# Attention and recurrent layer: output stores shared between two queues, weights split in halves, one gated output split later

## The chip, the cores and the metric

The kernel runs on one core of a Trainium2 chip. The metric is the device time of one launch in microseconds. A core has TensorE (PE, matmuls; its weight loads are listed as PEld), VectorE (DVE), ScalarE (ACT), GpSimd (POOL) and SyncE (SP, which here only issues DMAs). Each engine works through its own instructions in the order in which they stand in the program, and waits for the others by semaphores.

## What is computed

One step of a decoder trunk over a prompt of 1024 tokens and 8 sample tokens, model width 1024. The trunk has two layers: a recurrent block and its MLP, then a sliding-window attention and its MLP. Every sub-layer is normed first and added to the residual stream. The two mixers, cut to what matters:

```python
def recurrent_block(x, h0, conv_prev, w_in, ...):
    gate, xr = jnp.split(x @ w_in, 2, axis=-1)
    xc, conv_new = causal_conv(xr, conv_prev, conv_w, conv_b)
    y, h_new = rg_lru(xc, h0, w_a, b_a, w_x, b_x, lam)      # sigmoid gates, then a scan over time
    return (y * jax.nn.gelu(gate)) @ w_out, h_new, conv_new

def qkv_heads(x, w_qkv, q_g, k_g):
    q, k, v = jnp.split(x @ w_qkv, ...)                      # 16 query heads, 4 key/value heads of 64
    return rms_norm(q, q_g), rms_norm(k, k_g), v

def sink_attention(q, k, v, dist, mask, sinks):              # window of 128 positions
    s = jnp.einsum('...qkgd,...skd->...kgqs', q, k) * (HEAD_DIM ** -0.5)
    s = jnp.where(mask, s - slopes * dist, NEG_INF)
    m = jnp.maximum(jnp.max(s, axis=-1, keepdims=True), sink)
    e = jnp.exp(s - m)
    p = e / (jnp.sum(e, axis=-1, keepdims=True) + jnp.exp(sink - m))
    return jnp.einsum('...kgqs,...skd->...qkgd', p, v)
```

## The kernel before

All 1032 tokens stand in the columns of tiles, 128 rows of the model width to a tile, so that one activation is eight tiles of 128x1032. A matmul works on a third of the columns (344, chunks c = 0, 1, 2). To keep float32 accuracy each operand is held as a rounded part and a remainder (`hi`, `lo`; for weights `wh`, `wl`), and each product is three matmuls: hi by hi, lo by hi, hi by lo. So everything that PE reads is first split: ACT casts the rounded part (`act.copy`) and DVE subtracts it from the source to give the remainder.

**Weights.** They come in units of 128x1024. SP loads a unit into one of two raw buffers, ACT casts `wh` (L179), DVE makes `wl` (L180), which frees the raw buffer. `unit(n, j, ahead)` returns a unit and sees to it that the next `ahead` units are split as well. The first four units of the program are split in two halves of 512 columns, all others whole.

**Recurrent layer** (to about 335 us). `LRU` is a list written out by hand that sets the order of stages: x (projections of the recurrent branch), c (convolution), g (sigmoid gates of a block, L1309), r (Tanh, Exp, squares and scan), o (`gate_out`: projection of the gate branch, Gelu, product with the scanned y, and the split of the result into `goh` on ACT and `gol` on DVE, for the output projection). The stretch that matters reads `o0 o1 o3 g3 r3 o6 o2 o4 o7`. A scheduler orders instructions by their readiness and priority within each engine's queue, so code that is moved also moves neighbours. Sigmoid, Gelu, Sqrt and Exp make ACT load other tables (`ACT_TABLE_LOAD`).

**Attention** (about 985 to 1250 us). `proj_many` makes the first key and query tile, `v_proj` the values; the other seven query tiles and the second key tile are filler, put between the matmuls of attention. `q_evac` empties each chunk of a query tile (square on ACT, L839; `hi` L841, `lo` on DVE L842, then stored to four half tiles by SP). One step of attention: scores in a bank bS (L963), the biased minimum on DVE (L973), the exponential on ACT (`se`, L976), the reciprocal on DVE (L978), the scaling on GpSimd (L980), transposes on PE (L990) and their copy `pt` (L997), and the product with the values in bO (L1013). `stage_c` closes a group of four steps: for each of two head tiles, u = 0 and 1, ACT casts the output `o` (L1020), DVE makes its remainder (L1021), and for the first four head tiles (t < 4) both go to DRAM tensors `od` (od0h is the rounded part of head tile 0, od1l the remainder of head tile 1), to be loaded again for the output projection. There are eight such groups, with four stores each. `S` buffers (128x344) come from a ring of nine; a buffer is used again once everything that read it is done, a store included.

Of the kernel before, what the change touches and what calls it, by code (L numbers as in the profile page):

```python
# [65 lines left out]
def trunk(ctx: ExitStack, tc: tile.TileContext, I, O):  # L66
    nc = tc.nc
    pe, act, dve, pool, sp = nc.tensor, nc.scalar, nc.vector, nc.gpsimd, nc.sync
# [33 lines left out]
    def A2(s="a"):  # L102
        return ap.tile([P, TW], F32, tag="A", name=nm(s))

    def A(s="a"):
        return A2(s)[:, 0:T]
# [4 lines left out]
    def S(s="s"):  # L111
        return small["pool"].tile([P, CH], F32, tag="S", name=nm(s))
# [5 lines left out]
    def B(tag=None):  # L118
        if tag is None:
            tag = ring[turn[0] % len(ring)]  # L120
            turn[0] += 1
        return psum["pool"].tile([P, 512], F32, tag=tag, bufs=BANKS[tag], name=nm("b" + tag))
# [14 lines left out]
    def r_(x):  # L137
        return x.bitcast(F32R)

    def cs(c):  # L140
        return slice(c * CH, (c + 1) * CH)
# [11 lines left out]
    def V(n, m=0):  # L153
        o, _ = VEC[n]
        return vec[:, o + m:o + m + 1]
# [10 lines left out]
    def fetch(n):  # L166
        while len(raws) < min(n, len(units)):
            name, _, src, _ = units[len(raws)]
            if name[:2] == "dn":
                raws.append(small["pool"].tile([P, RQ[int(name[2])]], F32, tag="Q", name=nm("raw")))  # L170
            else:
                raws.append(R("raw"))
            sp.dma_start(raws[-1][:, 0:src.shape[1]], src)

    def split_unit(raw, alloc, eng, parts=1):
        hi, lo = alloc("wh"), alloc("wl")
        for q in range(parts):
            sl = slice(q * D // parts, (q + 1) * D // parts)
            act.copy(r_(hi[:, sl]), raw[:, sl])  # L179
            eng.tensor_tensor(r_(lo[:, sl]), raw[:, sl], hi[:, sl], ALU.subtract)  # L180
        return hi, lo
# [8 lines left out]
    for o in [("x", m) for m in range(4)] + LRU:  # L190
        if o[0] == "g":
            units.append(("gate", o[1], I["w_gate"][o[1]], W))
        elif o[0] in "xo":
            m = o[1] + (8 if o[0] == "x" else 0)
# [13 lines left out]
    nloaded = [0]  # L208

    def ensure(k):  # L210
        while nloaded[0] <= min(k, len(units) - 1):
            n, j, _, alloc = units[nloaded[0]]
            fetch(nloaded[0] + (NRAW[int(n[2])] if n[:2] == "dn" else 2))
            if alloc is None:
                loaded[(n, j)] = raws[nloaded[0]]
            else:
                loaded[(n, j)] = split_unit(raws[nloaded[0]], alloc, pool if nloaded[0] in (3, 13) else dve,
                                            2 if nloaded[0] < 4 else 1)
            nloaded[0] += 1

    def unit(n, j, ahead=2):
        k = index[(n, j)]
        for _ in range(ahead):
            if k + 1 < len(units) and units[k + 1][3] is not None:
                k += 1
        ensure(k)
        return loaded.pop((n, j))
# [26 lines left out]
    def proj(w, xs, **kw):  # L254
        ps = banks3()
        mm_group(ps, w, xs, range(NCH), **kw)
        return ps
# [8 lines left out]
    def split_act_dve(hi, lo, src, sl, eng=dve):  # L266
        act.copy(r_(hi[:, sl]), src)
        eng.tensor_tensor(r_(lo[:, sl]), src, hi[:, sl], ALU.subtract)
# [237 lines left out]
    class PairWeights:  # L506
# [13 lines left out]
        def source(self, key, name):  # L520
            kind, q = key
            if key not in self.src:
                n = f"{kind}{self.layer}"
                ensure(index[n, 2 * q + 1])
                xy = []
                for t in (loaded.pop((n, 2 * q)), loaded.pop((n, 2 * q + 1))):
                    w = P * (4 if kind == "up" else len(self.chunks[q // 4]))
                    xy += [t[0][:, 0:w], t[1][:, 0:w]] if isinstance(t, tuple) else [t[:, 0:w], t[:, w:2 * w]]
                self.src[key] = {"w": w, **dict(zip(("A21", "A11", "A12", "A22"), xy))}
            src = self.src[key]  # L530
            if name not in src:
                w = src["w"]
                x, y, op = SUMS[name]
                x, y = self.source(key, x), self.source(key, y)
                if name in ("S1", "S3"):
                    src[name, 1] = W("ws")
                src[name] = src[("S1" if name in ("S1", "S2") else "S3"), 1][:, slice(w, 2 * w) if name in ("S2", "S4") else slice(0, w)]
                dve.tensor_tensor(src[name], x, y, op)  # L538
            return src[name]
# [250 lines left out]
    def attention(hs):  # L790
# [114 lines left out]
        def vblk(b, p):  # L905
            h = b // 4
            o = (b % 4) * 256 + p * P
            return v_tiles[h][:, o:o + P]
# [91 lines left out]
        def stage_c(g):  # L1000
            t, b0 = STEPS[4 * g]
            p = t // 4
            op = B("O")
            for n in range(2):
                y = live.pop(("pt", 2 * g + n))
                b = b0 + n
                first = 1 if b == 0 else 0
                o = op[:, n * 256:n * 256 + 256]
                for h in range(first, 2):
                    x = vblk(b - 1 + h, p)  # L1010
                    for u in range(2):
                        r = slice(64 * u, 64 * u + 64)
                        pe.matmul(o[r, :], lhsT=x[:, r], rhs=y[:, (2 * h + u) * 256:(2 * h + u) * 256 + 256],  # L1013
                                  start=h == first, stop=h == 1, tile_position=(0, 64 * u))
            dst = slice(b0 * P, (b0 + 2) * P)
            for u in range(2):
                src = op.rearrange("p (b t q) -> p b t q", b=2, t=2)[:, :, u, :]
                x = [S("o")[:, 0:2 * P] for _ in range(2)] if t < 4 else [y[:, dst] for y in ohl[t + u]]
                hi, lo = [y.rearrange("p (b q) -> p b q", b=2) for y in x]
                last["o"] = act.copy(r_(hi), src).ins  # L1020
                dve.tensor_tensor(r_(lo), src, hi, ALU.subtract)  # L1021
                if t < 4:
                    for d, y in zip(od[t + u], x):
                        sp.dma_start(d[:, dst], y)

        kc, vc, zs = [], [], []

# [128 lines left out]
        for j in range(NJ):  # L1156
# [6 lines left out]
            n = max(0, int((j + 1 - j1) * r) - int((j - j1) * r)) if j < J0 or j >= J1 else 0  # L1163
            if j and j % 4 == 0:
                stage_c(j // 4 - 1)
# [9 lines left out]
            if J0 <= j < J0 + 4:  # L1175
                ensure(index["wo1", j - J0])
# [8 lines left out]
            if j == 52:  # L1185
                for t in range(4):
                    load_o(t, slice(2 * CH, SEQ))
        stage_c(NJ // 4 - 1)

        for _ in fill:  # L1190
# [107 lines left out]
    rr = {}  # L1298

    def gates(kb):  # L1300
        w = unit("gate", kb, 3)
        xk = [xcs[2 * kb], xcs[2 * kb + 1]]
        for mm in range(2):
            for g, b in ((0, "ba"), (1, "bx")):
                ps = proj(w, xk, col=lambda k: k * 512 + g * 256 + mm * P)
                o = A("ri")
                with tc.high_priority():
                    for c in range(NCH):
                        act.activation(o[:, cs(c)], ps[c], AF.Sigmoid, bias=V(b, 2 * kb + mm))  # L1309
                rr[2 * kb + mm, g] = o  # L1310
# [31 lines left out]
    def gate_out(m):  # L1342
        ps = proj(unit("in", m, 3 if ("o", m) != LRU[-1] else 0), hs)
        y = ys.pop(m)
        for c in range(NCH):
            g = S("g")
            dve.tensor_tensor(g, ps[c], rx[:, cs(c)], ALU.mult)
            act.activation(g, g, AF.Gelu_apprx_tanh)
            dve.tensor_tensor(y[:, cs(c)], y[:, cs(c)], g, ALU.mult)
        hi, lo = A("goh"), A("gol")  # L1350
        split_act_dve(hi, lo, y, slice(0, T))
        gos[m] = (hi, lo)

    stages = {"x": xr_stage, "c": conv, "g": gates, "r": recur, "o": gate_out}
    xr_first()
    for what, i in LRU:
        stages[what](i)
        if (what, i) == ("r", 3):
            sp.dma_start(O["states"], st)
    gl = [gos[m] for m in range(M8)]  # L1360
# [131 lines left out]
def _build(arrays):  # L1492
    import concourse.bacc as bacc

    nc = bacc.Bacc("TRN2", target_bir_lowering=False, num_devices=1)
    I = {n: nc.dram_tensor(n, a.shape, mybir.dt.from_np(a.dtype), kind="ExternalInput").ap() for n, a in arrays.items()}
    O = {n: nc.dram_tensor("o_" + n, s, F32, kind="ExternalOutput").ap() for n, s in _OUT_SHAPES.items()}
    with tile.TileContext(nc) as tc:
        trunk(tc, I, O)
    return nc  # L1500
# [23 lines left out]
```

## Time and profile before

| | us |
|---|---|
| median of 3 runs (1973.4 to 1975.09) | 1974.5 |
| the profiled execution | 1974.77 |
| its span, first to last instruction | 1973.0 |
| PE busy | 1959.7 |
| DVE busy | 1499.1 |
| ACT busy | 1007.2 |
| GpSimd busy | 357.4 |

A profile is one execution. A timeline row gives the start, the duration, the engine, the line, the operation and its tiles (out<-in), and in brackets how long the engine had stood idle before it and what ended that. `x4` folds four neighbours into one row. The mean granted clock of PE was 0.999.

### The profile page before, as it was taken

The page shows a single profiled execution, that of the slowest core. Times are in us where ns is not written, and L with a number is a line of the kernel's source. Part 1 is how long each engine was busy: PE and PEld are TensorE (multiplying, and loading weights), DVE is VectorE, ACT ScalarE, POOL GpSimd, SP SyncE. Part 2 cuts the span into 40 slices and gives each one's busy share as a digit, 9 for nine tenths or more (in the row PEclk, how much of TensorE's full clock was granted, in tenths as well). Part 3 has the DMA queues.
Part 4 walks back from the last instruction along what each step waited for, and adds up shares of the span by engine and source line. Part 5 has one row for each costly group of instructions (what it writes and reads, how often), then busy time and mean ns, then how long its engine had stood idle before and what let it go on. Part 6 is the DMA issues. An engine that isn't in the chain of part 4 may idle for free.

```text
span 1973.0 us, 34782 instructions
## 1 busy us (share of the span) xinstructions
PE 1959.7 (99%) x13004; PEld 1826.8 (93%) x13004; DVE 1499.1 (76%) x2996; ACT 1007.2 (51%) x1964; POOL 357.4 (18%) x614
## 2 busy tenths in 40 slices
PE   9999999999999999999999999999999999999999
PEld 8999999999999899999999897999999999999998
DVE  8996647987777888777846768579877779688784
ACT  6576535543434655544545657456443436455552
POOL 2220000000001233321005647100000003223321
PEclk9999999999999999999999999999999999999999
DMA  5111242244445798988344435612444447788877
GB/s 183 54 44 54 65 159 83 108 151 156 144 152 196 215 244 209 239 204 199 111 110 108 131 94 186 216 62 97 165 140 156 141 176 261 202 203 219 229 201 180
DMA packets 116441, 308.07 MB, mean 156 GB/s; under 512 B 17448, under 2 KB 47152, under 8 KB 116272
## 3 DMA queue, kind: packets, MB, share of 16 engines
q0 software_dynamic: 29472, 102.06, 21.6%
q1 hardware_dynamic: 58576, 133.44, 20.7%
q10 hardware_dynamic: 28224, 70.35, 10.0%
q8 instruction: 102, 1.67, 0.4%
q14 instruction: 67, 0.55, 0.1%
HBM read 177.95 MB, written 115.15 MB: 149 GB/s over the span
## 4 chain that ended last, share of the span: by engine, by line
PE 92%; DVE 3%; issue 2%; DMA 1%; ACT 1%; POOL 0%; SPq 0%; DVEq 0%; ACTq 0%; POOLq 0%
PE bD L570 35%; PE bZ L570 26%; PE bP L240 11%; PE bS L240 6%; PE bP L890 5%; PE bT L240 3%; PE bO L1013 2%; PE bS L963 1%; PE bS L920 1%; PE bT L990 1%; DVE xc L1281 1%; PE bP L990 1%; DMA x<-xT 0%; DVE wl L180 0%; PE bN L854 0%
## 5 line engine op out<-in xcount | busy, mean ns | idle before, releaser
L570 PEld LDWEIGHTS bD<-op,op 128*128 128x128 f32 x3072 | 380.5, 188 | 7.8
L570 PE MATMUL bD<-op,op 128*128 128x260 f32 x3072 | 383.0, 282 | 0.0
L570 PEld LDWEIGHTS bD<-tl,op 128*128 128x128 f32 x2880 | 362.3, 188 | 12.7 <-DVE ho L718 1.4
L570 PE MATMUL bD<-tl,op 128*128 128x260 f32 x2880 | 366.6, 282 | 0.8 <-DVE ho L718 0.7
L583 POOL DMA_DIRECT2D tl<-hsum x210 | 124.3, 670 | 892.8 <-PE bD L570 412.6
L417 ACT CAST op<-ws 128x512 fp32r<-128x512 f32 (+2 forms) x288 | 158.7, 560 | 248.8 <-DVE ws L538 123.2
L570 PE MATMUL bZ<-op,op 128*128 128x512 f32 x1152 | 282.2, 394 | 0.0
L570 PE MATMUL bZ<-tl,op 128*128 128x512 f32 x1080 | 272.0, 395 | 0.5 <-DVE tl L425 0.2
L570 PEld LDWEIGHTS bZ<-op,op 128*128 128x128 f32 x1152 | 210.5, 188 | 43.6 <-ACT he L704 0.4
L570 PEld LDWEIGHTS bZ<-tl,op 128*128 128x128 f32 x1080 | 194.3, 188 | 38.3 <-DVE tl L425 0.8
L425 DVE TENSOR_TENSOR tl<-tl 128x520 fp32r<-128x520 f32 (+1 forms) x210 | 136.5, 691 | 75.0 <-ACT tl L424 74.1
L417 ACT CAST op<-raw 128x512 fp32r<-128x512 f32 (+2 forms) x216 | 120.8, 561 | 135.0 <-PE bD L570 73.1
L418 DVE TENSOR_TENSOR op<-ws,op 128x512 fp32r<-128x512 f32 (+2 forms) x288 | 171.0, 609 | 9.7 <-ACT op L417 9.5
L418 DVE TENSOR_TENSOR op<-raw,op 128x512 fp32r<-128x512 f32 (+2 forms) x216 | 131.3, 609 | 9.7 <-ACT op L417 8.8
L718 DVE TENSOR_TENSOR ho<-bD,ho 128x520 f32<-128x520 f32 x140 | 97.3, 695 | 38.8 <-PE bD L570 37.2
L424 ACT CAST tl<-tl 128x520 fp32r<-128x520 f32 (+1 forms) x210 | 117.9, 626 | 3.8 <-DMA tl<-hsum 2.2
L708 DVE TENSOR_TENSOR ho<-bZ,ho 128x512 f32<-128x512 f32 x72 | 49.5, 687 | 44.6 <-PE bZ L570 44.3
L180 DVE TENSOR_TENSOR wl<-raw,wh 128x1024 fp32r<-128x1024 f32 (+1 forms) x53 | 61.4, 1166 | 27.2 <-ACT wh L179 17.6
L966 POOL TENSOR_SCALAR bias<-con,st 128x256 f32<-128x256 f32 (+1 forms) x128 | 64.3, 503 | 86.4 <-DVE den L973 46.9
L710 ACT COPY he<-bZ 128x512 f32<-128x512 f32 x68 | 39.9, 586 | 77.3 <-PE bZ L570 65.7
L692 ACT COPY he<-bZ 128x512 f32<-128x512 f32 x72 | 41.9, 582 | 71.4 <-PE bZ L570 65.0
L718 DVE TENSOR_TENSOR he<-bD,he 128x520 f32<-128x520 f32 x71 | 49.4, 695 | 38.1 <-PE bD L570 37.7
(347 smaller groups left out, 3941.6 us busy)
## 6 DMA issues: line engine op xcount, KB each, us to landing
raw<-w_up SPq DMA_DIRECT2D x64, 512.0 KB, 4.2
tl<-hsum POOLq DMA_DIRECT2D x120, 260.0 KB, 6.5
raw<-w_dn SPq DMA_DIRECT2D x64, 384.0 KB, 6.5
tl<-hsum POOLq DMA_DIRECT2D x90, 256.0 KB, 6.5
spill<-ho POOLq DMA_DIRECT2D x32, 516.0 KB, 6.7
spill<-he POOLq DMA_DIRECT2D x32, 516.0 KB, 6.4
hsum<-ts ACTq DMA_DIRECT2D x30, 520.0 KB, 3.7
hsum<-ho ACTq DMA_DIRECT2D x30, 516.0 KB, 3.5
```

What stands on the lines that cost most here:

```text
L180: eng.tensor_tensor(r_(lo[:, sl]), raw[:, sl], hi[:, sl], ALU.subtract)
L240: pe.matmul(o, lhsT=r_(wt[:, col(k):col(k) + P]), rhs=r_(xt[:, cs(c)]), start=(k == first and a == 0), stop=(k == final and a == 2))
L417: act.copy(r_(hi), x)
L418: dve.tensor_tensor(r_(lo), x, hi, ALU.subtract)
L424: act.copy(r_(hi), lo)
L425: eng.tensor_tensor(r_(lo), lo, hi, ALU.subtract)
L570: pe.matmul(d[:, 512 * b:512 * b + c], lhsT=r_(wt[:, j * P:j * P + P]), rhs=r_(xt[:, c * b:c * b + c]), start=first and j == 0 and a == 0, ...
L583: pool.dma_start(t[:, n:2 * n], src)
L708: dve.tensor_tensor(o0, d, o[:, HP], ALU.add)
L718: last["sum"] = dve.tensor_tensor(t, inner(d), t, ALU.add).ins
L890: pe.matmul(o, lhsT=r_(wt[:, k * P:k * P + P]), rhs=r_(xt[:, cs(c)]), start=(k == 0 and a == 0), stop=(k == M8 - 1 and a == 2))
L966: pool.tensor_scalar(bias2[:, o - n:o], distM[:, 256 - n:256], fac[:, t % 4, 1, b, u:u + 1], SLOPES[hd[u]], ALU.mult, ALU.mult)
```

## The change

1. In `stage_c` the two stores of the second head tile (u = 1: od1h, od1l, od3h, od3l) are issued by ACT, not SP. Those of u = 0 stay on SP.
2. The units of q, k, v and the output weights of the attention layer (`wo1`), 20 in all, are split in two halves of 512 columns.
3. The second gate block (kb = 1) asks for one unit ahead, not three.
4. For gate output 3 the split into `goh` and `gol` is put off until the next stage that isn't a gate output has been written, which is g3.

```diff
-                                            2 if nloaded[0] < 4 else 1)
+                                            2 if nloaded[0] < 4 or n in ("q", "k", "v", "wo1") else 1)
...
                     for d, y in zip(od[t + u], x):
-                        sp.dma_start(d[:, dst], y)
+                        (act if u else sp).dma_start(d[:, dst], y)
...
     def gates(kb):
-        w = unit("gate", kb, 3)
+        w = unit("gate", kb, 1 if kb == 1 else 3)
...
             dve.tensor_tensor(y[:, cs(c)], y[:, cs(c)], g, ALU.mult)
+        if m in (3,):
+            owed.append((m, y))
+        else:
+            gate_split(m, y)
+
+    def gate_split(m, y):
         hi, lo = A("goh"), A("gol")
         split_act_dve(hi, lo, y, slice(0, T))
         gos[m] = (hi, lo)
+
+    owed = []
...
         stages[what](i)
+        if what != "o" and owed:
+            gate_split(*owed.pop())
```

**At g3, on ACT.** Before, behind o3's three Gelus (L1348); `goh` is the cast of o3's output, `ri` are the sigmoids of g3, which empty PE's banks bP, bS and bT:

```order
L1348 ACTIVATE g_1976<-g_1976 128x344
L267 CAST goh_1980<-t_1211 128x1032
L1309 ACT_TABLE_LOAD
L1309 ACTIVATE ri_2011<-bP_1990,vec 128x344
L1309 ACTIVATE ri_2036<-bS_2015,vec 128x344
L1309 ACTIVATE ri_2011<-bP_1991,vec 128x344
```

Now the table load follows the Gelus:

```order
L1348 ACTIVATE g_1976<-g_1976 128x344
L1309 ACT_TABLE_LOAD
L1309 ACTIVATE ri_2007<-bP_1986,vec 128x344
L1309 ACTIVATE ri_2007<-bP_1987,vec 128x344
L1309 ACTIVATE ri_2007<-bP_1988,vec 128x344
```

and the cast stands behind the last of the twelve sigmoids, ahead of r3's Tanh (L1321) and Exp (L1323):

```order
L1309 ACTIVATE ri_2082<-bT_2063,vec 128x344
L267 CAST goh_2086<-t_1205 128x1032
L179 CAST wh_2230<-raw_2131 128x1024
L1321 ACTIVATE t_2093<-ri_2057,sp_333 128x1032
L1323 ACT_TABLE_LOAD
L1323 ACTIVATE ri_2057<-ri_2057,vec 128x1032
```

The sigmoids also stand in another order, one product after the other.

**At the norm ahead of the first key and query products, on ACT.** L306 to L308 are the norm's factor, `hh` the rounded parts of the normed activation, L839 the square of a query chunk. Before:

```order
L306 ACTIVATE q_10419<-bN_10410,vec 128x344
L179 CAST wh_10771<-raw_10763 128x1024
L307 ACTIVATE r_10418<-q_10419 128x344
L308 ACTIVATE q_10419<-r_10418 128x344
L839 ACTIVATE sq_10579<-bT_10639 128x344
L267 CAST hh_9874<-t_10425 128x344
```

Now:

```order
L306 ACTIVATE q_10419<-bN_10410,vec 128x344
L179 CAST wh_10779<-raw_10769 128x512
L307 ACTIVATE r_10418<-q_10419 128x344
L179 CAST wh_10779<-raw_10769 128x512
L308 ACTIVATE q_10419<-r_10418 128x344
L267 CAST hh_9874<-t_10425 128x344
L839 ACTIVATE sq_10585<-bT_10645 128x344
```

The cast of the weight is in two pieces, and the first `hh` has changed places with the square.

**At the fourth group of stores.** On ACT the group reads now as follows (before, the two DMA rows weren't there); `hi` is a query chunk, `se` an exponential:

```order
L1020 CAST o_12095<-bO_12080 128x256
L1024 DMA od1h<-o_12095 128x256
L1024 DMA od1l<-o_12096 128x256
L841 CAST hi_12173<-bP_12075 128x344
L976 ACTIVATE se_10474,den_10467<-se_10474,den_10467 128x257 x2
```

On DVE, a little later in the same place, before:

```order
L1021 TENSOR_TENSOR o_12233<-bO_12225,o_12232 128x256
L1021 TENSOR_TENSOR o_12239<-bO_12225,o_12238 128x256
L842 TENSOR_TENSOR lo_12252<-bP_12161,hi_12251 128x344
L973 ISA se_10475,den_10469<-bS_12246,bias_10473,nsink,st 128x256
L973 ISA den_10469 128x1
```

and now:

```order
L1021 TENSOR_TENSOR o_12253<-bO_12245,o_12252 128x256
L1021 TENSOR_TENSOR o_12259<-bO_12245,o_12258 128x256
L973 ISA se_10475,den_10469<-bS_12266,bias_10473,nsink,st 128x256
L973 ISA den_10469 128x1
L973 ISA se_10475,den_10469<-bS_12266,bias_10473,nsink,st 128x256
L973 ISA den_10469 128x1
L842 TENSOR_TENSOR lo_12272<-bP_12181,hi_12271 128x344
```

The remainder of the query chunk (L842) has moved behind the two softmax steps (L973).

## The prediction

> **What bounds the kernel now.** I read the page first, then the stretches, then the timeline where TensorE stands still.
>
> ```profile
> span 1973.0 us, 34782 instructions
> PE 1959.7 (99%) x13004; PEld 1826.8 (93%) x13004; DVE 1499.1 (76%) x2996; ACT 1007.2 (51%) x1964; POOL 357.4 (18%) x614
> 140.00:190.00 50.00, 50.00 (x319) 50.00 (x318) 40.08 (x59) 30.53 (x41) 0.83 (x2) 1.00 0.19 64
> 985.00:1005.00 20.00, 19.03 (x117) 18.02 (x115) 14.89 (x28) 12.13 (x26) 0.00 (x0) 1.00 0.25 80
> 1120.00:1140.00 20.00, 18.86 (x141) 17.35 (x141) 13.51 (x52) 11.30 (x36) 10.00 (x21) 1.00 0.61 174
> 1180.00:1200.00 20.00, 19.01 (x140) 15.84 (x139) 15.49 (x63) 13.55 (x43) 11.47 (x25) 1.00 0.60 171
> 1200.00:1220.00 20.00, 20.00 (x143) 16.84 (x144) 18.73 (x79) 13.83 (x44) 17.34 (x33) 1.00 0.66 221
> ```
>
> TensorE (PE) is busy 1959.7 of 1973.0 us, and the change leaves every matmul in place. So only what PE stands idle for can be won: 13.3 us in all. The stretches (start and end, length, then the busy time of PE, weight loads, VectorE, ScalarE, GpSimd) put about 1 us of it at each of three places that the change touches: 0.97 at 985, 1.14 at 1120 and 0.99 at 1180. Between 1200 and 1220 PE has no gap, but VectorE (DVE) is busy 18.73 of 20 us there. The rest of the change is worth what it does to those waits, or what new waits it makes.
>
> The profiled execution took 1974.77 us (span 1973.0 and 1.8 around it), 0.27 above the median of 1974.5. I sum against 1974.77 and take off 0.27 at the end.
>
> **The gate output that is split later (g3).** The rows are from the timeline of ScalarE (ACT) and of PE.
>
> ```profile
> 185.96 1.34 ACT L1348 ACTIVATE g<-g 128x344 f32<-128x344 f32 x3 [0.23 <-DVE g L1347]
> 188.03 1.06 ACT L267 CAST goh<-t 128x1032 fp32r<-128x1032 f32 x1 [0.73 <-DVE t L1349]
> 189.10 1.28 ACT L1309 ACT_TABLE_LOAD   x1
> 190.40 0.55 ACT L1309 ACTIVATE ri<-bP,vec 128x344 f32<-128x344 f32 x1
> 190.01 0.32 PE L240 MATMUL bT<-xch,wl 128*128 128x344 f32 x1
> 191.00 0.43 PE L240 MATMUL bP<-xch,wh 128*128 128x344 f32 x1 [0.67 <-ACT ri L1309]
> 191.26 0.32 PE L240 MATMUL bP<-xcl,wh 128*128 128x344 f32 x1
> 191.42 0.32 PE L240 MATMUL bP<-xch,wl 128*128 128x344 f32 x1
> ```
>
> ACT ends its Gelus at 187.30, waits 0.73 for DVE, casts for 1.06, loads a table for 1.28, and only then empties the first bank with a sigmoid. PE stood for that bank: matmuls of 344 columns start 0.16 apart (191.26, 191.42), so the one at 191.00 was due at 190.17 and is 0.83 late. With the cast behind all twelve sigmoids, the table load can follow the Gelus: 187.30 + 1.28 = 188.58, and the first sigmoid ends near 189.1, a microsecond before PE wants the bank. Gain 0.8; bounds 0 (another wait behind it) and 0.83. The moved cast and its DVE half now lie ahead of Tanh and Exp of r3, but that chain starts up to 1.8 us earlier (0.73 + 1.06), which covers them; the split gate output itself is first read in the output projection, after the remaining gate outputs. Uncovered, the cast would cost 1.06.
>
> **Weights one unit later (second gate block).** The cast that leaves the second gate block turns up later, between Exp and the squares of r2, where DVE waits for ACT:
>
> ```profile
> 136.91 1.05 ACT L179 CAST wh<-raw 128x1024 fp32r<-128x1024 f32 x1 [3.34 <-DMA raw<-w_in]
> 138.45 0.86 PE L240 MATMUL bP<-hh,wh 128*128 128x344 f32 x2 [0.37 <-ACT ri L1309]
> 152.84 2.65 DVE L1329 SCALAR_TENSOR_TENSOR t<-a,t 128x344 f32<-128x344 f32 x6 [4.13 <-ACT a L1328]
> ```
>
> The units stay in their order, each split in the place of its successor, so the cast at 136.91 will handle the unit before and wait for a load freed by the same DVE step; PE's wait at 138.45 stays. The extra cast, 1.05 like the one at 136.91, pushes r2's DVE chain back by up to as much. PE has no gap from 140 to 190, so the trace shows no slack and no lack of it. I take 0, with bounds of +1.05 and, if the wait at 138.45 goes, -0.37.
>
> **Weights of the attention layer in halves.** 20 units become two casts and two subtractions each. The place that matters is the norm ahead of the first key and query products:
>
> ```profile
> 988.46 0.55 ACT L306 ACTIVATE q<-bN,vec 128x344 f32<-128x344 f32 x1 [1.88 <-PE bN L277]
> 988.91 1.04 ACT L179 CAST wh<-raw 128x1024 fp32r<-128x1024 f32 x1
> 992.80 0.46 ACT L839 ACTIVATE sq<-bT 128x344 f32<-128x344 f32 x1 [1.94 <-PE bT L240]
> 993.15 1.23 ACT L267 CAST hh<-t 128x344 fp32r<-128x344 f32 x3
> 989.98 1.23 DVE L180 TENSOR_TENSOR wl<-raw,wh 128x1024 fp32r<-128x1024 f32 x1 [2.10 <-ACT wh L179]
> 993.75 1.36 DVE L268 TENSOR_TENSOR hl<-t,hh 128x344 fp32r<-128x344 f32 x3
> 992.45 0.32 PE L240 MATMUL bT<-hh,wl 128*128 128x344 f32 x1
> 993.68 0.58 PE L240 MATMUL bP<-hh,wh 128*128 128x344 f32 x2 [0.91 <-ACT hh L267]
> L417 ACT CAST op<-raw 128x512 fp32r<-128x512 f32 (+2 forms) x216 | 120.8, 561 | 135.0 <-PE bD L570 73.1
> L418 DVE TENSOR_TENSOR op<-raw,op 128x512 fp32r<-128x512 f32 (+2 forms) x216 | 131.3, 609 | 9.7 <-ACT op L417 8.8
> ```
>
> PE was due at 992.45 + 0.16 = 992.61 and is 1.07 late. In the new order the first cast hh stands ahead of the square of L839, so it can start at 992.80 instead of 993.15: 0.35 earlier. DVE's 1.23 becomes two pieces that can start half a cast sooner. But hl at 993.75 is close behind and PE needs it next; DVE sets that. I take 0.4, bounds 0 and 1.07. Two halves cost ACT 2 x 0.561 - 1.04 = 0.08 more per unit and DVE 2 x 0.609 - 1.23, nothing. Over 20 units that is 1.6 us of ACT, spread over stretches in which ACT is busy 11.3 to 13.8 of 20 us: no cost, and 1.6 without that cover.
>
> **Half of the output stores on ACT.** Sixteen of 32 stores leave SP's queue for ACT's. Rows of the timeline: SP, ACT, DVE, PE.
>
> ```profile
> 1116.27 2.62 SPq L877 DMA_DIRECT2D kl<-x  x4
> 1120.09 0.40 SPq L1024 DMA_DIRECT2D od1h<-o  x1
> 1114.93 0.37 ACT L1020 CAST o<-bO 128x256 fp32r<-128x256 f32 x1 [0.90 <-DVE o L1021]
> 1115.20 0.45 ACT L841 CAST hi<-bP 128x344 fp32r<-128x344 f32 x1
> 1115.37 0.42 DVE L1021 TENSOR_TENSOR o<-bO,o 128x256 fp32r<-128x256 f32 x1
> 1123.85 0.52 DVE L842 TENSOR_TENSOR lo<-bP,hi 128x344 fp32r<-128x344 f32 x1 [2.40 <-DMA od1h<-o]
> 1125.35 0.39 PE L963 MATMUL bS<-kh,q 128*128 128x256 f32 x1 [0.33 <-DVE den L973]
> 1128.76 0.39 PE L963 MATMUL bS<-kh,q 128*128 128x256 f32 x1 [0.81 <-DVE den L973]
> ```
>
> The piece stored as od1h is ready at 1115.30, but SP has key stores to issue first (the last four alone take 2.62, to 1118.89) and reaches it at 1120.09. Its buffer is wanted again by DVE's L842, which stands 2.40 us until 1123.85; behind it on DVE wait the softmax steps L973, and PE twice stands for them, 0.33 and 0.81. The idle time falls 0.16 short of a delay (0.67 listed against 0.83 at 191.00, 0.91 against 1.07 at 993.68), so the two make 0.33 + 0.81 + 2 x 0.16 = 1.5. In the new order ACT issues od1h right behind its cast, nearly 5 us earlier, and L973 stands ahead of L842. Both waits go: gain 1.5, bounds 0 and 1.5.
>
> What ACT pays: behind its second cast it issues one store, waits for DVE's remainder (1115.37 + 0.42 = 1115.79), and issues the next. The nearest ACT issue is
>
> ```profile
> L380 ACTq DMA_DIRECT2D spill<-y x48: 326/326/1086, 249.8 to 1330.8; - x48
> 1066.81 0.46 ACT L839 ACTIVATE sq<-bP 128x344 f32<-128x344 f32 x1 [0.48 <-PE bP L890]
> ```
>
> 0.33 each, so ACT is free at 1115.79 + 0.33 = 1116.12 instead of 1115.20: 0.9 us per group, 7.4 over eight groups. Queued behind are the cast hi, the exps and the copies pt of the transposed softmax tiles; DVE, GpSimd and PE wait for those in turn. Behind the first group ACT is idle 0.48 anyway. ACT has 5 us or more spare in these 20 us stretches and PE mostly runs behind it, so I charge 0.2 in all; bounds 0 and 7.4.
>
> [...]
>
> **The stop at 1197.**
>
> ```profile
> 1191.15 1.23 DVE L180 TENSOR_TENSOR wl<-raw,wh 128x1024 fp32r<-128x1024 f32 x1 [0.77 <-ACT wh L179]
> 1197.20 0.93 PE L990 MATMUL bT<-con,se 128*128 128x128 f32 x4 [0.93 <-POOL se L980]
> ```
>
> PE waits 0.93 at the end of a softmax chain through DVE, ACT and GpSimd. A weight in halves lets DVE start the first at about half the 0.77 it waits now. I take 0.5, bounds 0 and 0.93 + 0.16 = 1.09.
>
> **Sum.** -0.8 + 0 - 0.4 - 1.5 + 0.2 - 0.5 = -3.0: 1971.77 for an execution like the profiled one, 1971.5 as median.
>
> **Rivals.**
> - *Every touched wait goes.* 0.83 + 1.07 + 1.5 + 1.09 = 4.5 less, 1970.0, and 1969.5 if the wait at 138.45 goes as well. For: each has a named cause that the new order takes away. Against: hl close behind hh at 993.75, and the chain at 1197 has other links.
> - *The transfer, not its issue, holds the buffer, or DVE takes the gain back.* The store lands behind the key stores whoever issues it; or what was won is lost again at 1200 to 1220, where DVE has only 1.27 us spare. Then the 1.5 is missing: 1973.0.
> - *Slower: ACT's stores hold up softmax.* ACT takes its instructions in order, so a store that waits for DVE stops the exps behind it. The price is 0.9 us per group; with all of it on PE's path, and the sum's other terms of 1.7 kept without the 1.5, 7.4 - 1.7 = 5.7 more, 1980.2. It turns the sum positive once more than 3.2 / 8 = 0.4 us per group is uncovered. For: GpSimd and PE's transposes follow the exps closely (the 0.93 at 1197 is such a chain). Against: idle ACT behind the group at 1066. [...]
>
> **How the numbers follow.** Forecast 0.42, every wait gone 0.30, transfer or DVE 0.13, slower 0.15. A measurement of this kernel can tell about 0.2%, 3.9 us, from no change. Faster than 1970.6 takes the first rival and 0.12 of the forecast's share: 0.42. Slower than 1978.4 is mostly the last rival's: I give 0.11 to it and leave its other 0.04, with 0.30 and 0.13, within 0.2%: 0.47. The range runs from 1968.7, every wait gone and a microsecond more behind it, to 1976.5, where the stores cost about 5 us (2/3 of the bound) beside the other gains; beyond are about 0.06 below and 0.13 above.
>
> **What would show it.** Right: ACT's table load at g3 directly behind the Gelus and no wait of PE on ri near 190; no wait of DVE L842 on a store; PE busy 20.0 in the stretch that was 18.86. The halves are right if PE's wait before the first key product falls below 0.8. Wrong: PE waits on L973 or L980 right behind the store groups, ACT exps that start 0.5 us or more later than DVE's L973 ends, a new PE wait between 150 and 180, or L842 still waiting for a store that ACT issued early.

## The result, and the profile after

| | before | after |
|---|---|---|
| median of 21 runs each, us | 1974.68 | 1971.7 |
| lowest and highest, us | 1973.03, 1975.57 | 1970.23, 1976.66 |
| ratio, 95% interval | | 0.9987, 0.9981 to 0.9993 |

The highest run of after is one whose mean granted clock was 0.997; the other twenty had 0.999 or 1.0. The changed kernel is 3.0 us faster (by the interval 1.4 to 3.8), less than the 3.9 us that the prediction named as the bound for telling it from no change. From the page of after, and its stretches with the columns of the prediction:

```profile
PE 1959.2 (99%) x13004; PEld 1826.8 (93%) x13004; DVE 1500.5 (76%) x3016; ACT 1008.8 (51%) x1984; POOL 358.3 (18%) x614
985.00:1005.00 20.00, 19.25 (x119) 18.11 (x118) 14.21 (x28) 11.99 (x28) 0.00 (x0) 1.00 0.27 86
1120.00:1140.00 20.00, 20.00 (x153) 18.95 (x152) 15.03 (x60) 12.76 (x40) 11.96 (x24) 1.00 0.52 148
1180.00:1200.00 20.00, 19.02 (x140) 15.13 (x138) 15.76 (x67) 13.07 (x41) 12.18 (x27) 1.00 0.65 188
```

Of the three gaps in these stretches one has closed (PE 18.86 before, 20.00 now), one has shrunk a little (19.03, now 19.25), one is as it was (19.01, now 19.02).

To see what each place gave, I set every PE instruction of one trace beside the same instruction of the other, wherever PE had done the same work up to it, and took the difference of their starts. How much that difference grows over a stretch is what the stretch gave. Where nothing was changed it moves too. Over the second feed-forward layer after gains 0.4 and the stores alone 1.3, of which 0.9 is one wait of PE at 1728 that some executions have and others don't. Over the first, after loses 0.6 in many small pieces; every kernel with all the parts loses 0.5 to 0.8 there and the stores alone lose nothing, so this belongs to the kernel, and its cause is open. Single places are good to a tenth or two, the sum of an execution is not. Gains against before, in us (stretches by the start in before):

| stretch | predicted | after | stores alone | halves alone | late split alone |
|---|---|---|---|---|---|
| 187 to 214, g3 | 0.8 | 0.94 | 0.03 | 0.03 | 1.04 |
| 975 to 995, norm ahead of keys and queries | 0.4 | 0.17 | 0 | 0.18 | 0 |
| 1104 to 1110 | not foreseen | -0.44 | -0.43 | -0.74 | 0 |
| 1124 to 1134, the store group | 1.5 less 0.2 | 1.63 | 1.68 | 0.13 | -0.35 |
| 1195 to 1199, the stop | 0.5 | 0 | 0 | 0 | 0 |
| 1234 to 1246 | not foreseen | 0.57 | 0 | 0.54 | 0 |

The places in after sum to 2.9. **g3**, timeline of ACT, to be read against the prediction's rows at 185.96 to 190.40; PE has no wait left between 185 and 194:

```profile
185.60 1.34 ACT L1348 ACTIVATE g<-g 128x344 f32<-128x344 f32 x3 [0.23 <-DVE g L1347]
186.96 1.28 ACT L1309 ACT_TABLE_LOAD   x1
188.25 1.43 ACT L1309 ACTIVATE ri<-bP,vec 128x344 f32<-128x344 f32 x3
```

The table load stands directly behind the Gelus, and the sigmoids start 2.65 us behind the first Gelu (188.25 - 185.60) where it was 4.44 before (190.40 - 185.96): 1.8 earlier.

**The norm ahead of keys and queries**, PE and DVE:

```profile
992.37 0.58 PE L240 MATMUL bP<-hh,wh 128*128 128x344 f32 x2 [0.44 <-ACT hh L267]
993.26 0.42 PE L240 MATMUL bP<-hl,wh 128*128 128x344 f32 x1 [0.31 <-DVE hl L268]
989.46 0.69 DVE L180 TENSOR_TENSOR wl<-raw,wh 128x512 fp32r<-128x512 f32 x1 [0.21 <-ACT wh L179]
990.07 0.57 DVE L309 SCALAR_TENSOR_TENSOR q<-bN,vec,q 128x344 f32<-128x344 f32 x1
```

PE's one wait of 0.91 for hh has become 0.44 for hh and 0.31 for hl: cast earlier, but VectorE's remainder hl close behind it. DVE's first step of the norm (L309) starts at 990.07, and at 991.12 before; 0.9 of these 1.05 us is that the whole trace runs ahead here, and what is left is about the 0.17 of the table.

**The store group**, ACT and DVE:

```profile
1113.66 0.33 ACTq L1024 DMA_DIRECT2D od1h<-o  x1
1114.53 0.45 ACT L841 CAST hi<-bP 128x344 fp32r<-128x344 f32 x1 [0.90 <-DVE o L1021]
1122.10 0.45 ACT L841 CAST hi<-bP 128x344 fp32r<-128x344 f32 x1 [1.81 <-DMA q<-hi]
1121.48 0.54 DVE L973 CUSTOM_DVE_ANT_0 se<-bS,bias,nsink 128x256 f32<-128x256 f32 x1
1122.58 0.52 DVE L842 TENSOR_TENSOR lo<-bP,hi 128x344 fp32r<-128x344 f32 x1 [0.55 <-ACT hi L841]
```

ACT issues od1h right behind its cast and pays 0.90 in this group, the price the prediction gave. DVE's wait of 2.40 for a store is gone. In its place ACT waits 1.81 for another store (of a query piece, q) before it casts the next hi; but DVE's softmax steps L973 (1121.48) now stand ahead of L842 (1122.58), and PE doesn't wait.

**The stop**, PE, then DVE's last read for the tile's exps, then ACT; first after, then before:

```profile
1194.90 0.93 PE L990 MATMUL bT<-con,se 128*128 128x128 f32 x4 [0.92 <-POOL se L980]
1192.43 0.08 DVE L973 DVE_READ_ACCUMULATOR2_ANT den<- 128x1 f32 x1
1192.74 0.27 ACT L306 ACTIVATE q<-bN,vec 128x16 f32<-128x16 f32 x1 [0.39 <-PE bN L854]
1193.41 0.49 ACT L976 ACTIVATE se<-se,den 128x257 f32<-128x257 f32 x1
```

```profile
1194.80 0.09 DVE L973 DVE_READ_ACCUMULATOR2_ANT den<- 128x1 f32 x1
1195.04 0.27 ACT L306 ACTIVATE q<-bN,vec 128x16 f32<-128x16 f32 x1 [0.39 <-PE bN L854]
1195.72 0.49 ACT L976 ACTIVATE se<-se,den 128x257 f32<-128x257 f32 x1
```

DVE is done at 1192.5, and the exps (L976) begin at 1193.41, because three small steps of the last query norm (L306 to L308) stand ahead of them in ACT's queue and the first of these waits 0.39 for PE's norm sums. It was so before: DVE done at 1194.9, the same 0.39, the exps at 1195.72.

**The two stretches that nobody had foreseen** show no wait of PE. What differs is the order of its matmuls. The products with the values (L1013) are issued in runs. The kernel writes them in pairs, u = 0 and u = 1 of one step, which fill the two halves of the rows of bO. Four rows of after, then five of before:

```profile
1075.59 1.95 PE L1013 MATMUL bO<-pt,vt 128*64 128x256 f32 x16
1103.74 1.94 PE L1013 MATMUL bO<-pt,vt 128*64 128x256 f32 x14
1105.61 0.85 PE L817 MATMUL bN<-sq,con 128*128 128x344 f32 x2
1106.38 0.65 PE L1013 MATMUL bO<-pt,vt 128*64 128x256 f32 x2
```

```profile
1198.06 0.65 PE L1013 MATMUL bO<-pt,vt 128*64 128x256 f32 x4
1108.27 0.32 PE L890 MATMUL bP<-hl,wh 128*128 128x344 f32 x1
1108.52 1.08 PE L1013 MATMUL bO<-pt,vt 128*64 128x256 f32 x8
1109.53 0.43 PE L890 MATMUL bP<-hh,wl 128*128 128x344 f32 x1
1109.80 0.27 PE L990 MATMUL bT<-con,se 128*128 128x128 f32 x1
```

*Pairs that are split.* A run of 14 takes as long as one of 16, and a run of 2 as long as one of 4. The starts of the single products in the trace say why: the run of 14 holds six pairs that start together and two products that start alone, and the run of 2 holds two more that start alone. A product alone takes as long as a pair: in the run of 14 the last whole pair starts at 1104.87 and the two alone at 1105.08 and 1105.30, 0.22 apart like the pairs ahead of them. Before, two runs of 8 whole pairs stood at 1104 in place of these 14 and 2: 1.94 + 0.65 - 2 x 1.08 = 0.43, the 0.44 that was lost. The stores alone and every later kernel with 14 and 2 there lose 0.42 to 0.44; the late split and the gate block alone keep 8 and 8 and lose nothing (all stores on ACT, with 8 and 8 between other neighbours, 0.12).

*The cost of a run.* From the start of the matmul ahead of the run of 8 to the start of the one behind it pass 1109.53 - 1108.27 = 1.26 us. Of these 0.16 is the matmul ahead, and 0.87 are the eight products (eight more take 1.95 - 1.08); 0.23 are left. The matmul behind takes 1109.80 - 1109.53 = 0.27 until the next start, 0.11 more than its 0.16. So a run costs some 0.3 us beside its products, which is neither a wait nor idle time in the profile. Each of these runs is of 128*64 between 128*128. That the change of tile is what costs is not shown: no run here takes it away. The halves alone have 6, 2 and 8 at 1104, one run more than 14 and 2 with as many pairs split, and lose 0.74: again 0.3 more.

Before at 1234, then after at the same products:

```profile
1234.78 1.08 PE L1013 MATMUL bO<-pt,vt 128*64 128x256 f32 x6
1236.37 0.65 PE L1013 MATMUL bO<-pt,vt 128*64 128x256 f32 x2
1237.85 1.08 PE L1013 MATMUL bO<-pt,vt 128*64 128x256 f32 x8
```

```profile
1232.49 1.08 PE L1013 MATMUL bO<-pt,vt 128*64 128x256 f32 x8
1235.12 1.08 PE L1013 MATMUL bO<-pt,vt 128*64 128x256 f32 x8
```

Three runs became two there, and two split pairs became whole (6 takes as long as 8): 0.65 by these rows, 0.57 by the starts.

### The profile page after: what moved, and what is told of

The parts are those of the page before. It is cut to its first block, busy times and chain, and to the rows that moved or that the text cites. A ratio compares the mean times of both kernels' runs of the same rounds, so it can differ in the third digit from the quotient of the medians.

```text
span 1969.5 us, 34826 instructions
## 1 busy us (share of the span) xinstructions
PE 1959.2 (99%) x13004; PEld 1826.8 (93%) x13004; DVE 1500.5 (76%) x3016; ACT 1008.8 (51%) x1984; POOL 358.3 (18%) x614
## 4 chain that ended last, share of the span: by engine, by line
PE 96%; DVE 2%; DMA 1%; ACT 0%; issue 0%; POOL 0%; SPq 0%; DVEq 0%; ACTq 0%
PE bD L570 36%; PE bZ L570 26%; PE bP L240 12%; PE bS L240 7%; PE bP L890 5%; PE bT L240 3%; PE bS L963 2%; PE bO L1013 2%; PE bS L920 1%; PE bT L990 1%; DVE xc L1281 1%; PE bP L990 1%; DMA x<-xT 0%; PE bN L854 0%; DVE wl L180 0%
## 5 line engine op out<-in xcount | busy, mean ns | idle before, releaser
L180 DVE TENSOR_TENSOR wl<-raw,wh 128x512 fp32r<-128x512 f32 (+1 forms) x73 | 64.5, 898 | 33.8 <-ACT wh L179 16.8
L973 DVE CUSTOM_DVE_ANT_0 se<-bS,bias,nsink 128x256 f32<-128x256 f32 (+1 forms) x128 | 63.6, 521 | 22.0 <-PE bP L990 9.3
```

The lines of the kernel that those rows point to most:

```text
L973: dve.tensor_tensor_reduce(se[:, u, 256 - n:256], s[:, u * 256:u * 256 + n], bias2[:, o - n:o], scale=fac[:, t % 4, 0, b, u:u + 1], scalar ...
```

## The experiments

My theory behind the result: the store part works by the queue that issues, not by ACT; g3 works by ACT's order; the stop at 1195 is ACT's order too; and the two unforeseen stretches come from the order of PE's matmuls. The expectations put a price of 0.4 us on each run, which counted in the matmul ahead, and did not look at pairs. The rivals are those of the prediction: the transfers, and ACT's time. Edits of the first four are against the kernel before, of the others against the changed kernel. Results are medians in us; ratios are against the kernel before on the same chip. For each of the four parts alone, and for all stores on ACT, the interval holds 1.0: there the total settles nothing, and the reading rests on the traces.

**One part at a time.** Stores alone:

```diff
-                        sp.dma_start(d[:, dst], y)
+                        (act if u else sp).dma_start(d[:, dst], y)
```

> Only the stores: od of u = 1 issued by ACT, the rest as before. Theory (the late issue on SP is what held the S buffer): PE's two waits on L973 near 1125 and 1129 go, 1.5 to 1.7 us less between 1115 and 1130, DVE's 2.40 us wait in L842 goes; about 1973.0 against 1974.6. Rival (the transfer holds the buffer): L842 or its neighbours still wait 1 us or more and PE loses 0.5 or more there. Rival (ACT's stores hold up softmax): the gain is used up by new PE waits behind the eight groups, the time is 1974.5 or more. The trace of the changed kernel shows PE 0.4 us later over 1075 to 1110, the first four groups; if the stores cause that, it shows here too.

Measured 1972.53 (0.9993, 0.9984 to 1.0001). The store group gives 1.68 by itself, with no wait on L973, and -0.43 at 1104 comes with it, in the same order of runs as in after.

Halves alone:

```diff
-                                            2 if nloaded[0] < 4 else 1)
+                                            2 if nloaded[0] < 4 or n in ("q", "k", "v", "wo1") else 1)
```

> Only the 20 weight units of the attention layer in halves. Theory: PE's delay ahead of the first key and query products shrinks by 0.2 to 0.4 us (993.68 before), the stop at 1197 stays near 0.9, the waits near 1125 stay; some of the 0.9 us won between 1216 and 1242 in the changed kernel shows here, if it is due to the halves of the output weights. About 1974.0. Rival (the extra instructions cost ACT and DVE where they are short): PE loses up to 0.5 us between 1180 and 1240, about 1975.

Measured 1973.81 (0.9997, 0.9989 to 1.0006). The norm gives 0.18, so hl takes back what hh gives here too. The stop stays. The gain at 1234 belongs to this part.

The late split alone:

```diff
-        hi, lo = A("goh"), A("gol")
-        split_act_dve(hi, lo, y, slice(0, T))
-        gos[m] = (hi, lo)
+        if m in (3,):
+            owed.append((m, y))
+        else:
+            gate_split(m, y)
...
+        if what != "o" and owed:
+            gate_split(*owed.pop())
```

> Only the split of gate output 3 put off. Theory: PE's 0.83 us wait on the sigmoids at 191 goes and nothing takes its place; 0.8 to 0.95 us less from 185 on, about 1973.7. Rival (the third gate block's earlier unit order is needed too): a wait of 0.3 us or more on ACT or on a weight appears between 185 and 215, and the time is 1974.3 or more.

Measured 1974.02 (1.0, 0.9991 to 1.0009): 1.04 at g3 and no wait left there. Its store group, untouched, is 0.35 worse than that of before: in before DVE's wait there ended with a landing (2.40 for od1h), and the group differs by that much between these two executions.

The gate block alone:

```diff
-        w = unit("gate", kb, 3)
+        w = unit("gate", kb, 1 if kb == 1 else 3)
```

> Only the second gate block asking for one unit ahead instead of three. Theory: nothing on PE's path, all its waits between 60 and 335 as before (about 1 us near 72, 1.2 near 138, 0.9 near 191); 1974.6 within 0.5. Rival: the extra cast between Exp and the squares of r2 shows as a PE wait of 0.3 to 1.0 us between 150 and 180, 1975.0 to 1975.6; or the wait at 138 changes by 0.3 or more.

Measured 1974.0 (0.9998, 0.9989 to 1.0007). The wait at 138 is there as before (0.43 for ri), no new one between 150 and 180: the 0 of the prediction.

**Another queue than ACT's, and twice the share.**

```diff
-                        (act if u else sp).dma_start(d[:, dst], y)
+                        (pool if u else sp).dma_start(d[:, dst], y)
```

> The changed kernel with the stores of u = 1 on GpSimd's queue in place of ACT's. Theory (what counts is only that SP's queue no longer holds them back): PE's two waits on L973 near 1125 to 1129 stay away here too, as in the changed kernel; a GpSimd issue takes some 0.7 us against 0.33, and GpSimd scales the softmax tiles, so up to 1 us may be lost behind a group: 1971.5 to 1973. Rival (ACT's queue itself gives the gain, for instance by holding ACT back): the waits near 1125 to 1129 come back, 1973.3 or more.

Measured 1971.44 (0.9985, 0.9975 to 0.9994), with 1.64 at the store group (after 1.63). What helped was leaving SP's queue; ACT is not special. The four issues by GpSimd from 1115 to 1122 take 0.55 to 0.59 each, where ACT takes 0.33 for od1h in after. DVE of this run:

```profile
1121.04 0.52 DVE L842 TENSOR_TENSOR lo<-bP,hi 128x344 fp32r<-128x344 f32 x1
1121.47 0.54 DVE L973 CUSTOM_DVE_ANT_0 se<-bS,bias,nsink 128x256 f32<-128x256 f32 x1
```

L842 stands ahead of L973 here, as it did before the change, and doesn't wait. So the gain doesn't need the other order of L842 and L973; the earlier issue is enough. (At 1104 this run has 6, 2 and 8 and loses 0.74.)

```diff
-                        (act if u else sp).dma_start(d[:, dst], y)
+                        act.dma_start(d[:, dst], y)
```

> The changed kernel with all 32 output stores on ACT, none on SP: ACT's share of the stores doubled. Theory (ACT's issue time of 0.33 is covered): no PE wait on L973 or L980 behind the eight groups; any difference comes from another order on PE, at most 0.6 either way: 1971.1 to 1972.4. Rival (ACT's stores hold up softmax, price 0.9 us per group and up): PE waits of 0.3 us or more appear behind the groups, 1973 to 1978.

Measured 1972.98 (0.9993, 0.9984 to 1.0002), 1.3 more than after and outside the expected range, a miss. 1.7 is lost between 1116 and 1121. PE and ACT of this run:

```profile
1119.44 0.43 PE L890 MATMUL bP<-hh,wh 128*128 128x344 f32 x1 [0.92 <-DVE lo L842]
1114.17 0.33 ACTq L1024 DMA_DIRECT2D od0h<-o  x1
1116.29 0.33 ACTq L1024 DMA_DIRECT2D od1h<-o  x1
1118.00 0.35 ACTq L1024 DMA_DIRECT2D od1l<-o  x1
1118.39 0.45 ACT L841 CAST hi<-bP 128x344 fp32r<-128x344 f32 x1 [2.28 <-DMA od0h<-o]
1118.73 0.51 ACT L976 ACTIVATE se<-se,den 128x257 f32<-128x257 f32 x1
```

The first store is issued at 1114.17, right behind its cast. The fourth, od1l, has its data from DVE at 1116.06 and the issue ahead of it is done at 1116.62, but ACT issues it at 1118.00: the profile puts ACT's 2.28 ahead of the cast hi down to the landing of od0h, and 1118.00 is 3.83 behind that store's issue, so I take it that od1l's issue waited for that landing. The cast hi and the exps stand behind it in ACT's queue, though the L973 steps of these exps were done by 1117.8; DVE's L842 needs hi, and PE waits for it. So with twice the share the slower rival does come true in this group, by this reading: the store that waits in ACT's queue holds up what is behind it. Whether hi needed the buffer of od0h besides is not shown. By the same reading the transfer took no less from ACT's queue than od1h took from SP's before (1120.09 to 1123.85, 3.76). In the change issue time was the bound, and 1.63 came of it.

**The runs of products with values**, broken up to 32 from the 25 of after:

```diff
-                        pe.matmul(o[r, :], lhsT=x[:, r], rhs=y[:, (2 * h + u) * 256:(2 * h + u) * 256 + 256],
-                                  start=h == first, stop=h == 1, tile_position=(0, 64 * u))
+                        with tc.high_priority():
+                            pe.matmul(o[r, :], lhsT=x[:, r], rhs=y[:, (2 * h + u) * 256:(2 * h + u) * 256 + 256],
+                                      start=h == first, stop=h == 1, tile_position=(0, 64 * u))
```

> The changed kernel with the products with the values (L1013) at high priority, which breaks them into 32 runs of at most 8 matmuls; the changed kernel has 25 runs, of up to 16. Theory (each run costs PE about 0.4 us beside its matmuls: a run of 16 takes 2.13 us, one of 8 takes 1.27): 7 x 0.41 = 2.9 us more between 1060 and 1250, without PE waiting for anyone: about 1974.6. Rival (the differences of 0.4 to 0.6 us at 1106 and 1237 were short waits that the profile doesn't show): no more than 1 us more, or a gain from products that start earlier: 1970.7 to 1972.7.

Measured 1976.35 (1.0011, 1.0002 to 1.002), 4.65 more than after where 2.9 was expected. The order does two things here. All pairs are whole, which saves 0.43 at 1104 and as much at 1090, where after has another 2 and 14. And there are more runs: by 1195, 20 where after has 12, for the same 148 products. By then it has lost 3.65 against after, about 0.56 of it at the one wait of PE (0.40 listed, for a copy of ACT's, and the 0.16 that a listed wait falls short). The other 3.1 and the 0.9 saved make 4.0 for eight runs: 0.5 each, where the rows above gave 0.3. Another 0.95 goes to waits from 1200 to 1212. So the sign is the theory's, but the price of a run is not one number: 0.3 at 1104 and 0.5 here, and why is open. The profiled execution took 1978.02, 1.7 more than the median, and that shows a thing of its own. PE of this run, then its stretches there (PE's granted clock is the third column from the end):

```profile
1201.38 0.33 PE L990 MATMUL bP<-con,se 128*128 128x128 f32 x1 [1.22 <-POOL se L980]
1203.28 1.98 PE L1014 MATMUL bO<-pt,vt 128*64 128x256 f32 x8
```

```profile
1202.00:1203.00 1.00, 0.89 (x6) 0.69 (x4) 1.00 (x5) 0.26 (x1) 1.00 (x3) 0.74 0.89 206
1203.00:1204.00 1.00, 1.00 (x6) 0.53 (x6) 0.95 (x6) 0.34 (x2) 0.82 (x3) 0.50 0.88 270
1204.00:1205.00 1.00, 1.00 (x6) 0.24 (x2) 0.05 (x2) 0.00 (x0) 0.91 (x3) 0.50 1.02 345
1205.00:1206.00 1.00, 1.00 (x7) 0.82 (x5) 0.30 (x1) 0.70 (x3) 0.00 (x0) 0.55 0.91 227
```

The clock fell to half for some 3.5 us: a run of 8 took 1.98 instead of 1.08. 0.26 + 0.50 + 0.50 + 0.45 = 1.7 us lost, all of what this execution is over the median.

**What was left on the table.** Three edits at once: the exps ahead of L306 at the stop; the cast ahead of the sigmoids at 138 moved behind them; the last weights ahead of the norm at 990 to GpSimd. `exps` lists the exps as they are issued, `last["ri"]` is the latest sigmoid, and `issue_after` holds what it encloses behind the instruction named.

```diff
-                loaded[(n, j)] = split_unit(raws[nloaded[0]], alloc, pool if nloaded[0] in (3, 13) else dve,
+                loaded[(n, j)] = split_unit(raws[nloaded[0]], alloc, pool if nloaded[0] in (3, 13, index["q", 1]) else dve,
...
-            rstd_m2(st, r, 2 * NB)
+            if t == 7:
+                with tc.issue_after(exps[-5]):
+                    rstd_m2(st, r, 2 * NB)
+            else:
+                rstd_m2(st, r, 2 * NB)
...
-        w = unit("gate", kb, 1 if kb == 1 else 3)
+        w = unit("gate", kb, {1: 1, 2: 2}.get(kb, 3))
...
-        ps = proj(unit("in", m, 3 if ("o", m) != LRU[-1] else 0), hs)
+        if m == 5:
+            with tc.issue_after(last["ri"]):
+                w = unit("in", m, 3)
...
```

> The changed kernel with three further edits, each at a place where PE still waits: the weight casts ahead of o5 queued behind the sigmoids of g2; in the factors of the last query tile, ACT's L306 to L308 queued behind the two exponentials at 1193; the remainder of the second query weight made by GpSimd, away from DVE's chain at 990. Theory: PE's wait at 138 (0.6 + 0.28 + 0.28) goes, 1.0 to 1.2 us; the one at 1195 (0.92) shrinks by 0.5 to 0.9; those at 992 and 993 (0.6 and 0.5) shrink by 0.2 to 0.4: 1969.4 to 1970.2. Rival (each wait has a second cause close behind the first): less than 0.8 in all, 1971 or more.

Measured 1970.53 (0.9979, 0.997 to 0.9988), between what the theory and its rival said. The stop gave 0.84. The wait at 138 went (1.2 by 165), but 0.8 was lost at 172 to a new wait for g. At the norm 0.4 was lost. GpSimd and DVE of this run, then the same DVE step in after:

```profile
988.71 2.55 POOL L180 TENSOR_TENSOR wl<-raw,wh 128x512 fp32r<-128x512 f32 x2 [56.36 <-ACT wh L179]
990.50 1.12 DVE L311 SCALAR_TENSOR_TENSOR r<-q,r 128x344 f32<-128x344 f32 x1
```

```profile
990.67 0.52 DVE L311 SCALAR_TENSOR_TENSOR r<-q,r 128x344 f32<-128x344 f32 x1
```

The same step takes 1.12 beside GpSimd's subtraction and 0.52 without it: of the two subtractions that DVE was spared (0.69 each in after) it paid 0.60 back in this step.

So the next three leave GpSimd out. The stop alone (the second hunk above, with `exps`):

> The changed kernel with one edit: the first of the three small ScalarE steps of the last query norm (L306) waits until ScalarE has issued the first exps of the softmax tile before it. If ScalarE's order, and not VectorE's splits, made TensorE's 0.92 us stop near 1195, the stop goes and about 0.8 us is won: 1970.9. Rival: the norm's factors, now later, are missed by VectorE's next query tile, and TensorE loses the 0.8 again before 1220: 1971.7.

Measured 1970.4 (0.9982, 0.9973 to 0.9991). 1.01 gained at 1195 and kept: the rival falls, and the stop was ACT's order. ACT of this run has the exps first (line numbers are 5 higher):

```profile
1192.29 0.51 ACT L981 ACTIVATE se<-se,den 128x257 f32<-128x257 f32 x1
1193.29 0.26 ACT L306 ACTIVATE q<-bN,vec 128x16 f32<-128x16 f32 x1
```

The stop and the cast at 138 (hunks two to four above):

> The same, and the cast of the weights of the unit at 137 us moved behind the sigmoids of the second gate block, but without the weights of the attention layer's second query block on GpSimd, which cost 0.4 in the run of three edits. Theory: the 0.84 at 1195 and the net 0.35 at 137 to 187 stay, 0.4 at 990 is not lost: about 1.2 us under the changed kernel, 1970.5. Rival: what is won in the recurrent layer is lost again at 172 in full: 1970.9.

Measured 1970.42 (0.9982, 0.9973 to 0.999). As expected: 1.15 won by 165, 0.83 lost by 187.

The same with the gate block as it was before the change:

```diff
-        w = unit("gate", kb, 1 if kb == 1 else 3)
+        w = unit("gate", kb, 2 if kb == 2 else 3)
```

> As the run before, but with the second gate block loading as far ahead as before the change (that part of the change undone). If the wait of 0.78 us that turned up at 172 came from VectorE's share of the weights being split there, it goes, the 1.17 won at 137 stays, and the time is about 1.9 us under the changed kernel: 1969.8. Rival: the splits in the place where they stood before cost r2 a wait or bring 172 back: 1970.5 or later.

Measured 1969.69 (0.9976, 0.9966 to 0.9985): the fastest of all. It is 4.4 us under before on its own chip (1974.12), where the change is 3.0 under before on another; the two ratios' intervals just overlap, so that it beats the change is likely and not shown by the totals. The 1.20 won at 138 stays. Why, from ACT and DVE, first with the gate block changed (the run before), then with it undone:

```profile
151.11 1.03 ACT L179 CAST wh<-raw 128x1024 fp32r<-128x1024 f32 x1
152.18 1.23 DVE L180 TENSOR_TENSOR wl<-raw,wh 128x1024 fp32r<-128x1024 f32 x1 [3.88 <-ACT wh L179]
153.32 2.65 DVE L1334 SCALAR_TENSOR_TENSOR t<-a,t 128x344 f32<-128x344 f32 x6
```

```profile
151.68 2.65 DVE L1334 SCALAR_TENSOR_TENSOR t<-a,t 128x344 f32<-128x344 f32 x6 [3.98 <-ACT a L1333]
```

The cast and subtraction that the change puts there push r2's chain back by 153.32 - 151.68 = 1.64 us, and by some 2.2 counted from the same work of PE, since that trace runs 0.5 ahead here. In the changed kernel PE's wait at 138 covers that; once the wait is gone, PE waits at 172 instead.

## Why the prediction was right, and where it was not

- **g3, 0.8.** Measured 0.94, by the mechanism given; alone 1.04. The bound of 0.83 was a tenth or two short.
- **Gate block, 0.** Right, and the reason for doubt too: the upper bound named r2's DVE chain, and the last two runs show it to be 1.6 to 2.2 late, more than the 1.05 of that bound. It costs nothing only as long as the wait at 138, which the prediction left in place, stands ahead.
- **Norm, 0.4.** Measured 0.17. The step that was mis-sized is "I take 0.4": the prediction named hl as the next to be late and did not take it off. DVE's second half at 989.46 stands right ahead of the norm's steps, and those came only some 0.15 sooner, so hl came no sooner than that.
- **Stores, 1.5 less 0.2.** Measured 1.63, by the mechanism given, as the run on GpSimd's queue shows; ACT's 0.9 in the group traced is covered wholly: 0.2 too much was charged.
- **The stop, 0.5.** Measured 0; this step failed. "A weight in halves lets DVE start the first at about half the 0.77" took DVE's wait as a link of the chain, when the last link ahead of the exps was ACT's own queue. The exps' start should have been set against DVE's end in the trace of before, and then against what ACT had done in between; the run with the exps first showed it.
- **"The change leaves every matmul in place."** All are there, but in another order, and order has a price that PE's idle time doesn't show: pairs of products that are split, and runs between other tiles. It came to -0.44 and +0.57. So the bound "only what PE stands idle for can be won" was wrong as well.

The misses add up to -0.23 at the norm, -0.5 at the stop, 0.13 for the order; the gains beyond the terms to 0.14 at g3 and 0.33 at the stores. That they nearly cancel is luck: the median of 1971.7 meets 1971.5, but a time that came out with one of six terms failed, one at less than half of its size, and two effects that were not in the sum owes part of it to chance.

The rivals: not every wait went. The transfer did not hold the first store's buffer, nor did DVE take the gain back behind 1200. The slower case, ACT's stores holding up softmax, did not come in the change; with twice the share it did, in the one group where, as I read ACT's 2.28, a store waited in its queue for the landing of another, and cost 1.7. One sign that the prediction named for it, exps 0.5 us or more behind DVE's L973, is there at the stop (0.9), but it was there before (0.8) and comes from L306.

## What to carry to other kernels

Before you shorten the work ahead of a wait, find what stood last in the queue of the engine that ends it: a step of 0.3 us that is queued ahead of the right one, and itself waits, can be the whole stop. When a scheduler orders the instructions, compare the bound engine's own order, and count how often it goes from 128*128 to 128*64 products and back (0.3 to 0.5 us a run here) and whether products that start in pairs still do (one alone took a pair's 0.22), even if no instruction was added. A part that costs nothing beside a wait should be weighed again once that wait is removed.

## What the runs showed of the hardware

- Two 128*64 products that fill the two halves of a bank's rows took PE as long together as one alone: runs of 14 and 16 took 1.94 and 1.95, runs of 2 and 4 took 0.65 each. The profile counts the difference as busy.
- A run of 128*64 matmuls between 128*128 ones cost some 0.3 us (0.5 in the kernel with broken runs) that the profile counts as busy.
- PE's granted clock fell to 0.50 for about 3.5 us at 1202 in one execution of the kernel with broken runs, behind a wait of 1.22 that ended at 1201.38; behind the wait of 0.92 that ended at 1194.90 in after it stayed at 1.00. What made it fall is not shown.
- One DVE step with both inputs in SBUF (L311) took 1.12 instead of 0.52 beside a GpSimd subtraction, while L309, with one input in PSUM, took 0.58 beside it and 0.57 without. Why is not shown.
- With all stores on ACT, and SP issuing key stores beside it (2.72 and 2.56 for four each), ACT's 2.28 ahead of a cast ended, by the profile, with the landing of a 128x256 store; another store behind it in ACT's queue was issued 3.83 after it.
